# A decoder trunk's weight streams: which gate pairs take seven products, where the single weight block lies, and the order of a product's last pair

## The chip, the cores and the metric

The kernel runs on one core of one Trainium2 chip. The metric is the device time of one execution in microseconds (us), lower is better. A matrix product here is done by TensorE (PE), the weights are prepared by ScalarE (ACT) and VectorE (DVE), GpSimd (POOL) does a few element-wise steps, and SyncE (SP) issues the transfers.

## The reference

One layer of a decoder, 256 tokens, width D = 2048, all in float32. In short:

```python
h = rms_norm(x, mix_norm)
proj = h @ w_in                      # q, k, v of two attentions, LRU, SSM, and 4 * 2048 gate columns
branches = [dilated(proj), lru(proj), sliding(proj), ssm(proj)]      # four mixers, 768 wide each
merged = sum(sigmoid(gate_b) * (branch_b @ w_branch[b]) for b in range(4))
x2 = x + merged @ w_out
u = rms_norm(x2, ffn_norm)
out = x2 + (silu(u @ w_gate) * (u @ w_up)) @ w_ffn_out               # hidden width 5632
```

## The kernel before, in words

The 256 tokens are two blocks t = 0, 1 of 128. Weights come once from HBM, 1 MB at a time. The activations stand in SBUF transposed, each split into a high and a low part; every weight block is split likewise: ACT writes the high part `wh` (L209) and DVE the rest `wl` (L214). One product of a weight block with an activation block is three matmuls of 128x128 by 128x512 (L202 high by high, L203 high by low weight, L204 low by high weight).

`stream_pairs` multiplies by two column blocks n = 0, 1 of 512, so a product has four results (n, t), each one bank of PSUM. A pair p is one 1 MB transfer: two row blocks k = 0, 1 of the two column blocks. `plan` is the order of the pairs. An ordinary pair makes two weight blocks a (k = 0) and b (k = 1) of 128x1024 and does eight products, `for k, n, t`. A pair in `seven` does seven products in their place, in the manner of Strassen and Winograd: from the raw weights DVE makes a sum t13 (L227, `ws`) and two more sums (L233, L234), and the weight blocks are a (one block, 128x512), b, c (of t13) and d (of the last two sums), each 128x1024 but a. The seven products go to three of the four result banks and to four shared banks m1, m5, m7, m6, which are added in at the end of the pairs of that kind (`shared_products`). The operands on the activation side (`hs_hi`, `hs_lo` for the gates, from `input_sums`; `xs` and `sx` for the FFN) are formed once.

Raw weights have 3 buffers, `whi` and `wlo` 4 each, whatever the block's size. A slot comes free when the last product with its block is done.

The last pair of every product is done bank by bank, so that bank (0,0) is finished first, then (0,1), (1,0), (1,1):

```python
                order = [(k, n, t) for k in range(2) for n in range(2) for t in range(T)]
                if i == len(plan) - 1:
                    order = [(k, n, t) for n in range(2) for t in range(T) for k in range(2)]
```

PSUM has eight banks: `psm` holds two tiles of two banks, `psx` four single banks (tag `mps`). A product in `psm` takes both of the two tiles, one for each n, so the next one in `psm` needs the same four banks again. A dependence goes by the tile: a read of one bank of a tile waits for both, and the next product's first matmul in a tile waits for the reads of both.

The stages in the order of time: start, SSM, LRU and attention projections up to 587 us; eight gates (c = 0, 1, four mixers each), each followed by its branch product of three pairs (in `psx` banks), to 1062.9; `w_out` (`stream`) to 1154.7; eleven products of the first FFN matrix (`w_ffn_in`, j = 0 to 10, 43.2 us each); two products of the second one (`w_ffn_out`, c = 0 from 1630.1, c = 1 from 1750.1). The gate product is read by DVE at L973, the branch at L983, the FFN-in product at L1078 (n = 0) and L1082 (n = 1), the second matrix's at L1145. Eight pairs a gate; eight pairs, two of them with seven products, in an FFN-in product; 22 pairs, eight with seven products, in one of the second matrix.

The gates use `PLAN_GATE`: gate (0, 0) has no pair of seven, (0, 1) and (1, 0) have a plan of their own, the five others take the pairs in order 0 to 7; seven gates have pairs 1, 3, 5 with seven products.

The order on each engine is set by Tile's scheduler, ahead of the run. The weights' loads, splits and sums stand in `tc.high_priority(offset=4000)`, the reads of the banks don't. Between pairs `pump()` advances side work (transposes, sums, loads of operands) held in two queues, near and far, as generators.

Two small tables are loaded among the constants at the start: `tri`, a mask of the SSM, and `onehot`, the distance table from which `bias_vector` makes the attention bias with one matmul.

Of the kernel before, what the change touches and what calls it, by code (L numbers as in the profile page):

```python
# [10 lines left out]
F32 = mybir.dt.float32  # L11
F32R = mybir.dt.float32r
AF = mybir.ActivationFunctionType
ALU = mybir.AluOpType
# [4 lines left out]
P = 128  # L19
D = 2048  # L20
S = 256
T = S // P
# [4 lines left out]
KG = 2  # L27
# [10 lines left out]
UNITS = [("c", 0), ("c", 1)] + [("a", h) for h in range(6)]  # L38
LINE = 512
SB_LOW, SB_TOP = 16512, 212960  # L40
CONST = 4640
SEVEN_GATE = (1, 3, 5)
PLAN_GATE = {(0, 0): (range(8), ()), (0, 1): ((0, 2, 1, 4, 3, 6, 5, 7), SEVEN_GATE), (1, 0): ((0, 2, 1, 4, 3, 6, 5, 7), SEVEN_GATE)}
SEVEN_IN = (3, 5)
SEVEN_OUT = list(range(1, 16, 2))
PLAN_OUT = ([0, 2, 4, 6, 1, 8, 3, 10, 5, 12, 7, 14, 9, 16, 11, 17, 13, 18, 15, 19, 20, 21], list(range(22)))
# [36 lines left out]
def hybrid(ctx, tc, a):  # L83
    nc = tc.nc
    V, A, G, PE = nc.vector, nc.scalar, nc.gpsimd, nc.tensor
# [8 lines left out]
    wp = ctx.enter_context(tc.tile_pool(name="wp", bufs=4))  # L94
    actp = ctx.enter_context(tc.tile_pool(name="actp", bufs=1))
    const = ctx.enter_context(tc.tile_pool(name="const", bufs=1))
    pad("pad_c", -CONST % LINE)
    psm = ctx.enter_context(tc.tile_pool(name="psm", bufs=2, space=PSUM))
# [3 lines left out]
    def ctile(shape, name, src=None, dt=F32):  # L102
        t = const.tile(shape, dt, name=name, tag=name)
        if src is not None:
            nc.sync.dma_start(t, src)
        return t

    def mps(name):
        return psx.tile([P, 512], F32, name=name, tag="mps")
# [16 lines left out]
    def pump():  # L126
        for queue in side.values():
            advance(queue)
# [45 lines left out]
    def stream_pairs(src, offset, plan, hi, lo, seven, name, mid=None, pool="psm"):  # L174

        if pool == "psm":  # L180
            two = [psm.tile([P, T, 512], F32, name=f"ps_{name}_{n}", tag="psmain") for n in range(2)]
            c = [[two[n][:, t] for t in range(T)] for n in range(2)]
        else:
            c = [[mps(f"ps_{name}_{n}{t}") for t in range(T)] for n in range(2)]
        m = {}
        left, begun = {}, set()

        def banks(p):
            if p in seven:
                return ["m1", (0, 0), (1, 0), "m5", "m7", "m6", (0, 1)]  # L190
            return [(n, t) for _ in range(2) for n in range(2) for t in range(T)]

        for p in plan:
            for b in banks(p):
                left[b] = left.get(b, 0) + 1

        def product(b, x, w, z):
            xh, xl = x
            wh, wl = w
            out = m[b] if b in m else c[b[0]][b[1]]  # L200
            left[b] -= 1
            PE.matmul(out, xh, wh[:, z], start=b not in begun, stop=False)  # L202
            PE.matmul(out, xh, wl[:, z], start=False, stop=False)  # L203
            PE.matmul(out, xl, wh[:, z], start=False, stop=left[b] == 0)  # L204
            begun.add(b)

        def high(x, z0, z1, nm):
            wh = wp.tile([P, KG, 512], F32R, name=f"wh_{nm}", tag="whi")
            A.activation(wh[:, z0:z1], x, AF.Copy)  # L209
            return x, z0, z1, wh, nm  # L210

        def low(x, z0, z1, wh, nm):
            wl = wp.tile([P, KG, 512], F32R, name=f"wl_{nm}", tag="wlo")
            V.tensor_tensor(wl[:, z0:z1], x, wh[:, z0:z1].bitcast(F32), op=ALU.subtract)  # L214
            return wh, wl

        sevens = [i for i, p in enumerate(plan) if p in seven]
        for i, p in enumerate(plan):
            with tc.high_priority(offset=4000):
                raw = wp.tile([P, 4, 512], F32, name=f"wr_{name}_{p}", tag="wraw", bufs=RAW)  # L220
                o = offset + p * P * 4 * 512
                nc.sync.dma_start(
                    raw, bass.AP(tensor=src.tensor, offset=src.offset + o, ap=[[4 * 512, P], [512, 4], [1, 512]])
                )
                if p in seven:
                    t13 = pools["sum"].tile([P, 2, 512], F32, name=f"ws_{name}_{p}", tag="wsum")
                    V.tensor_tensor(t13, raw[:, 1:3], raw[:, 0:1].to_broadcast([P, 2, 512]), op=ALU.add)  # L227
                    h11 = high(raw[:, 1:2], 1, 2, f"{name}_{p}a")
                    h2 = high(raw[:, 2:4], 0, 2, f"{name}_{p}b")
                    h13 = high(t13, 0, 2, f"{name}_{p}c")  # L230
                    w11 = low(*h11)
                    w2 = low(*h2)
                    V.tensor_tensor(raw[:, 0], t13[:, 1], raw[:, 1], op=ALU.add)  # L233
                    V.tensor_tensor(raw[:, 1], raw[:, 3], raw[:, 0], op=ALU.add)  # L234
                    h24 = high(raw[:, 0:2], 0, 2, f"{name}_{p}d")
                    w13 = low(*h13)
                    w24 = low(*h24)
                else:
                    w1 = low(*high(raw[:, 0:2], 0, 2, f"{name}_{p}a"))
                    w2 = low(*high(raw[:, 2:4], 0, 2, f"{name}_{p}b"))  # L240

            def x(k, t):
                return hi[:, 2 * p + k, t * P : (t + 1) * P], lo[:, 2 * p + k, t * P : (t + 1) * P]

            if p in seven:
                if not m:
                    m = {b: mps(f"{b}_{name}") for b in ("m1", "m5", "m7", "m6")}
                s = [(h[0][:, h[2], j], h[1][:, h[2], j]) for h in (seven[p],) for j in range(3)]
                product("m1", x(0, 0), w11, 1)
                product((0, 0), x(1, 0), w2, 1)  # L250
                product((1, 0), x(0, 1), w2, 0)
                product("m5", s[0], w13, 0)
                product("m7", s[2], w13, 1)
                product("m6", s[1], w24, 0)
                product((0, 1), x(1, 1), w24, 1)
                if i == sevens[-1]:
                    mid(m)
            else:
                order = [(k, n, t) for k in range(2) for n in range(2) for t in range(T)]
                if i == len(plan) - 1:  # L260
                    order = [(k, n, t) for n in range(2) for t in range(T) for k in range(2)]
                for z, (k, n, t) in enumerate(order):
                    product((n, t), x(k, t), (w1, w2)[k], 1 - n)
                    if z == 3 and pool == "psm" and not (sevens and sevens[0] < i < sevens[-1]):
                        pump()
            if i < len(plan) - 1 and pool == "psm" and not (sevens and sevens[0] <= i < sevens[-1]):
                pump()
        return c
# [79 lines left out]
    for kind, j, sl in chunk_plan():  # L348
        n = sum(w for _, w in sl)
# [12 lines left out]


    ident = ctile([P, P], "ident", a["ident"])
    tri = ctile([P, P], "tri", a["tri"])
    ones = ctile([P, P], "ones")
    V.memset(ones, 1.0)
    scw = ctile([P, 10, 5], "scw", a["conv_ssm"])
# [24 lines left out]
    tabx = ctile([36, 24], "tabx")  # L393
    nc.sync.dma_start(tabx[0:32, :], a["rel_bias_table"])
    nc.sync.dma_start(tabx[32:36, :], a["group_neg"])
    onehot = ctile([36, 384], "onehot", a["onehot"])
    bvec = dram.tile([24, 384], F32, name="bvec", tag="bvec")

    def bias_vector():
        bps = mps("bias_ps")  # L400
        PE.matmul(bps[:24, :384], tabx, onehot, start=True, stop=True)
        bsb = aq.tile([P, 512], F32, name="bsb", tag="tok", bufs=3)
        V.tensor_copy(bsb[:24, :384], bps[:24, :384])
        nc.sync.dma_start(bvec, bsb[:24, :384])
        yield
# [42 lines left out]
    aq = att1.enter_context(tc.tile_pool(name="aq", bufs=1, side="right"))  # L448
# [3 lines left out]
    sp_ = ssd.enter_context(tc.tile_pool(name="sp_", bufs=1, side="right"))  # L452
# [24 lines left out]

    zz = sp_.tile([P, T, BW], F32, name="zz", tag="zz")
    dtx = sp_.tile([P, T, 12], F32, name="dtx", tag="dtx")
    xbcT = sp_.tile([P, 10, S + 3], F32, name="xbcT", tag="xbcT")  # L480
    V.memset(xbcT[:, :, 0:3], 0.0)
    cv = sp_.tile([P, 10, S], F32, name="cv", tag="cv")
# [267 lines left out]
    pools = {}  # L750
# [168 lines left out]
    order = (1, 3, 2, 0)  # L919
# [25 lines left out]
    def input_sums():  # L945
        for i, p in enumerate(SEVEN_GATE):
            s3 = slice(2 * p, 2 * p + 2)
# [7 lines left out]
    for c in range(2):  # L955
        mg = gmp.tile([P, 2, T, 512], F32, name=f"mg{c}", tag="mg")
        for ib, b in enumerate(order):
            g4 = gmp.tile([P, 2, T, 512], F32, name=f"gt{c}{b}", tag="gt")
            gt = [[g4[:, n, t] for t in range(T)] for n in range(2)]
            if (c, ib) == (0, 1):  # L960
                mtp_stack, mT_hi, mT_lo = close_attention()
                hp = pools["sum"] = hsum.enter_context(tc.tile_pool(name="hp", bufs=1, side="right"))
                hs_hi, hs_lo = (hp.tile([P, len(SEVEN_GATE), 3, P], F32R, name=f"hs_{x}", tag=f"hs_{x}") for x in ("hi", "lo"))
                later(input_sums(), "far")
            plan, sv = PLAN_GATE.get((c, ib), (range(8), SEVEN_GATE))
            sv = {p: (hs_hi, hs_lo, SEVEN_GATE.index(p)) for p in sv}
            gps = stream_pairs(
                win, gate_off + (c * 4 + ib) * D * 1024, plan, actA_hi, actA_lo, sv, f"g{c}{b}", lambda m, gt=gt: shared_products(m, gt)
# [117 lines left out]
    n = len(SEVEN_OUT)  # L1086
# [159 lines left out]
```

## Time and profile before

| | |
|---|---|
| time, median of 3 runs | 1870.43 us (1869.89 to 1871.45) |
| time of the profiled execution | 1871.93 us |
| span of the profiled execution | 1870.2 us |
| mean granted TensorE clock | 0.999 |
| TensorE matmuls busy | 1854.8 us |
| VectorE busy | 1429.9 us |
| ScalarE busy | 970.6 us |
| HBM traffic | 195 GB/s over the span |

The span is the stretch from the first to the last instruction that the profiler recorded; the execution's own time is a little longer. A row of busy time counts how long instructions of an engine were open. Matmuls overlap one another, so the sum over matmuls is longer than what each adds to the end; the starts of one after another tell that.

### The profile page before, as it was taken

The numbers are of one execution on the slowest core, as the hardware profiler recorded it, in microseconds if no ns is written. First come the engines' busy times: TensorE is split into PE (matmuls) and PEld (weight loads), VectorE is DVE, ScalarE is ACT, GpSimd is POOL, SyncE is SP. The second block draws the span as 40 slices with busy tenths as digits, with TensorE's granted clock in tenths as the row PEclk, the third lists the DMA queues.
The fourth block names the chain that finished last, engine by engine and source line by source line (L and its number), as shares of the span: only waits on it lengthen the run. The fifth ranks groups of instructions, "written<-read, shape, count | busy, mean of one in ns | idle before, by whom it ended". The sixth has DMA issues, their size and how long they took to land.

```text
span 1870.2 us, 22270 instructions
## 1 busy us (share of the span) xinstructions
PE 1854.8 (99%) x8537; PEld 1543.9 (83%) x8537; DVE 1429.9 (76%) x1766; ACT 970.6 (52%) x1220; POOL 175.1 (9%) x152
## 2 busy tenths in 40 slices
PE   8999999999999999999999999999999999999998
PEld 8988888888888888888888888888888888878887
DVE  6867876565555788888888766888888888888885
ACT  6645655444444455555555554555555555455553
POOL 0032422222122001110011100000000000000000
PEclk9999999999999999999999999999999999999999
DMA  8644454455444455455556656445555555555653
GB/s 297 208 158 154 179 198 174 166 180 187 168 178 169 173 196 199 187 190 216 196 197 226 222 180 225 185 185 209 204 188 213 213 196 198 195 207 217 247 196 142
DMA packets 64392, 365.47 MB, mean 195 GB/s; under 512 B 7904, under 2 KB 19484, under 8 KB 23196
## 3 DMA queue, kind: packets, MB, share of 16 engines
q1 hardware_dynamic: 64284, 364.04, 53.1%
q8 instruction: 67, 1.10, 0.2%
q14 instruction: 41, 0.34, 0.1%
HBM read 358.21 MB, written 5.80 MB: 195 GB/s over the span
## 4 chain that ended last, share of the span: by engine, by line
PE 93%; DVE 3%; issue 2%; DMA 2%; ACT 0%; POOL 0%; DVEq 0%; POOLq 0%; ACTq 0%
PE ps_fi L202 7%; PE ps_fi L204 7%; PE ps_fi L203 7%; PE ps_att L169 6%; PE ps_att L167 6%; PE ps_att L168 6%; PE ps_g L202 5%; PE ps_g L204 5%; PE ps_g L203 5%; PE ps_fo L202 3%; PE ps_fo L203 3%; PE ps_fo L204 3%; PE ps_b L204 2%; PE ps_b L202 2%; PE ps_b L203 2%
## 5 line engine op out<-in xcount | busy, mean ns | idle before, releaser
L161 DVE TENSOR_TENSOR wl_att<-wr_att,wh_att 128x1024 fp32r<-128x1024 f32 x128 | 159.6, 1250 | 92.5 <-ACT wh_att L159 92.3
L159 ACT ACTIVATE wh_att<-wr_att 128x1024 fp32r<-128x1024 f32 x128 | 135.4, 1059 | 163.9 <-PE ps_att L169 145.3
L167 PE MATMUL ps_att<-wh_att,hT_hi 128*128 128x512 f32 x512 | 206.3, 403 | 0.0
L169 PE MATMUL ps_att<-wh_att,hT_lo 128*128 128x512 f32 x512 | 200.0, 391 | 0.0
L168 PE MATMUL ps_att<-wl_att,hT_hi 128*128 128x512 f32 x512 | 199.5, 390 | 0.0
L169 PEld LDWEIGHTS ps_att<-wh_att,hT_lo 128*128 128x128 f32 x512 | 96.1, 188 | 20.7
L168 PEld LDWEIGHTS ps_att<-wl_att,hT_hi 128*128 128x128 f32 x512 | 96.4, 188 | 19.0
L167 PEld LDWEIGHTS ps_att<-wh_att,hT_hi 128*128 128x128 f32 x512 | 96.3, 188 | 18.8
L985 POOL TENSOR_TENSOR mg<-mg,gt 128x512 f32<-128x512 f32 x24 | 38.7, 1642 | 434.3 <-DVE gt L983 434.3
L167 PE MATMUL ps_ssm<-wh_ssm,hT_hi 128*128 128x384 f32 (+2 forms) x160 | 57.2, 358 | 7.0 <-ACT hT_hi L312 7.0
L161 DVE TENSOR_TENSOR wl_o<-wr_o,wh_o 128x1024 fp32r<-128x1024 f32 x32 | 40.8, 1281 | 24.8 <-ACT wh_o L159 24.7
L159 ACT ACTIVATE wh_o<-wr_o 128x1024 fp32r<-128x1024 f32 x32 | 33.8, 1061 | 47.0 <-PE ps_o L169 38.6
L790 POOL TENSOR_TENSOR sq_t<-tk_t 128x512 f32<-128x512 f32 (+3 forms) x32 | 32.5, 1025 | 272.2 <-ACT tk_t L785 271.9
L168 PE MATMUL ps_ssm<-wl_ssm,hT_hi 128*128 128x384 f32 (+2 forms) x160 | 56.7, 355 | 0.6 <-DVE wl_ssm L161 0.6
L169 PE MATMUL ps_ssm<-wh_ssm,hT_lo 128*128 128x384 f32 (+2 forms) x160 | 56.5, 353 | 0.0
L167 PE MATMUL ps_o<-wh_o,mT_hi 128*128 128x512 f32 x128 | 50.8, 397 | 0.0
L169 PE MATMUL ps_o<-wh_o,mT_lo 128*128 128x512 f32 x128 | 50.0, 390 | 0.0
L168 PE MATMUL ps_o<-wl_o,mT_hi 128*128 128x512 f32 x128 | 49.8, 389 | 0.0
L159 ACT ACTIVATE wh_ssm<-wr_ssm 128x768 fp32r<-128x768 f32 (+2 forms) x40 | 35.2, 889 | 26.9 <-PE ps_ssm L169 16.9
L161 DVE TENSOR_TENSOR wl_ssm<-wr_ssm,wh_ssm 128x768 fp32r<-128x768 f32 (+2 forms) x40 | 40.2, 1012 | 9.9 <-ACT wh_ssm L159 9.7
L159 ACT ACTIVATE wh_lru<-wr_lru 128x1024 fp32r<-128x1024 f32 x24 | 25.4, 1059 | 29.2 <-PE ps_lru L169 21.0
L167 PE MATMUL ps_lru<-wh_lru,hT_hi 128*128 128x512 f32 x96 | 39.3, 409 | 0.0
(1235 smaller groups left out, 5622.0 us busy)
## 6 DMA issues: line engine op xcount, KB each, us to landing
wr_fi<-in_w_ffn_in SPq DMA_DIRECT2D x88, 1024.0 KB, 4.8
wr_att<-in_w_in SPq DMA_DIRECT2D x64, 1024.0 KB, 4.7
wr_g<-in_w_in SPq DMA_DIRECT2D x64, 1024.0 KB, 4.8
wr_fo<-in_w_ffn_out SPq DMA_DIRECT2D x44, 1024.0 KB, 4.9
wr_b<-in_w_branch SPq DMA_DIRECT2D x24, 1024.0 KB, 4.8
wr_o<-in_w_out SPq DMA_DIRECT2D x16, 1024.0 KB, 4.8
wr_lru<-in_w_in SPq DMA_DIRECT2D x12, 1024.0 KB, 4.8
wr_ssm<-in_w_in SPq DMA_DIRECT2D x8, 768.0 KB, 6.5
```

Source lines behind the costliest of these rows:

```text
L159: A.activation(wh, rk, AF.Copy)
L161: V.tensor_tensor(wl, rk, wh.bitcast(F32), op=ALU.subtract)
L167: PE.matmul(o_ps, xh, wh[:, kk], start=(k == 0), stop=False)
L168: PE.matmul(o_ps, xh, wl[:, kk], start=False, stop=False)
L169: PE.matmul(o_ps, xl, wh[:, kk], start=False, stop=(k == kc - 1))
L202: PE.matmul(out, xh, wh[:, z], start=b not in begun, stop=False)
L203: PE.matmul(out, xh, wl[:, z], start=False, stop=False)
L204: PE.matmul(out, xl, wh[:, z], start=False, stop=left[b] == 0)
L790: G.tensor_tensor(sq[:, :m], tok[:, :m], tok[:, :m], op=ALU.mult)
L985: G.tensor_tensor(mg[:, n, t], mg[:, n, t], gt[n][t], op=ALU.add)
```

## The change

Five edits.

1. Pair 7 joins pairs 1, 3 and 5: four of eight pairs have seven products in the seven gates that have such pairs. `input_sums` forms a fourth set of operands.
2. The plans change: (0, 1) and (1, 0) go 0, 2, 1, 3, 4, 5, 7, 6; the five other gates go 1, 0, 3, 2, 5, 4, 7, 6. Each of these ends in an ordinary pair.
3. The single weight block (a of a pair of seven) gets one buffer of its own for its high part and one for its low part (`wh1`, `wl1`), in the gates and in both FFN matrices, instead of a slot of `whi` and `wlo`.
4. The last pair's own order goes: it is done like the others, weight block by weight block, in every product of `stream_pairs`.
5. `tri` and `onehot` leave the constants and are loaded later, into pools of the SSM and the attention; the constants shrink from 4640 to 2592 bytes.

```diff
-CONST = 4640
-SEVEN_GATE = (1, 3, 5)
-PLAN_GATE = {(0, 0): (range(8), ()), (0, 1): ((0, 2, 1, 4, 3, 6, 5, 7), SEVEN_GATE), (1, 0): ((0, 2, 1, 4, 3, 6, 5, 7), SEVEN_GATE)}
+CONST = 2592
+SEVEN_GATE = (1, 3, 5, 7)
+PLAN_GATE = {
+    (0, 0): (range(8), ()),
+    (0, 1): ((0, 2, 1, 3, 4, 5, 7, 6), SEVEN_GATE),
+    (1, 0): ((0, 2, 1, 3, 4, 5, 7, 6), SEVEN_GATE),
+}
...
-        def high(x, z0, z1, nm):
-            wh = wp.tile([P, KG, 512], F32R, name=f"wh_{nm}", tag="whi")
-            A.activation(wh[:, z0:z1], x, AF.Copy)
-            return x, z0, z1, wh, nm
+        def high(x, nm):
+            if x.shape[1] == 1:
+                wh = pools["sum"].tile([P, 1, 512], F32R, name=f"wh_{nm}", tag="wh1")
+            else:
+                wh = wp.tile([P, KG, 512], F32R, name=f"wh_{nm}", tag="whi")
+            A.activation(wh, x, AF.Copy)
+            return x, wh, nm
...
+        def low(x, wh, nm):
+            if x.shape[1] == 1:
+                wl = pools["sum"].tile([P, 1, 512], F32R, name=f"wl_{nm}", tag="wl1")
+            else:
+                wl = wp.tile([P, KG, 512], F32R, name=f"wl_{nm}", tag="wlo")
+            V.tensor_tensor(wl, x, wh.bitcast(F32), op=ALU.subtract)
             return wh, wl
...
-                product("m1", x(0, 0), w11, 1)
+                product("m1", x(0, 0), w11, 0)
...
                 order = [(k, n, t) for k in range(2) for n in range(2) for t in range(T)]
-                if i == len(plan) - 1:
-                    order = [(k, n, t) for n in range(2) for t in range(T) for k in range(2)]
...
-    tri = ctile([P, P], "tri", a["tri"])
...
-    onehot = ctile([36, 384], "onehot", a["onehot"])
...
     def bias_vector():
+        onehot = aq.tile([P, 512], F32, name="onehot", tag="tok", bufs=3)[:36, :384]
+        nc.sync.dma_start(onehot, a["onehot"])
+        yield
         bps = mps("bias_ps")
...
+    tri = sp_.tile([P, P], F32, name="tri", tag="tri")
+    nc.sync.dma_start(tri, a["tri"])
...
-            plan, sv = PLAN_GATE.get((c, ib), (range(8), SEVEN_GATE))
+            plan, sv = PLAN_GATE.get((c, ib), ((1, 0, 3, 2, 5, 4, 7, 6), SEVEN_GATE))
```

## Rows read from the trace of the kernel before

**Rows 1.** The page's busy times, share of the span, instructions.

```profile
PE 1854.8 (99%) x8537; PEld 1543.9 (83%) x8537; DVE 1429.9 (76%) x1766; ACT 970.6 (52%) x1220; POOL 175.1 (9%) x152
```

**Rows 2.** The waits of TensorE: us in total, times, longest.

```profile
PE ps_ssm L167 <- ACT hT_hi L312: 7.0, 1, 7.0
PE m_fo L203 <- DVE wl_fo_1d L214: 1.3, 1, 1.3
PE m_fo L202 <- ACT wh_fo_1d L209: 0.8, 1, 0.8
```

**Rows 3.** Windows: length, busy time of PE, PEld, DVE, ACT, POOL, granted clock, DMA share, GB/s.

```profile
946.00:1004.00 58.00, 57.72 (x255) 47.50 (x254) 48.09 (x49) 30.46 (x34) 6.39 (x5) 1.00 0.53 198
...
1154.00:1630.00 476.00, 476.00 (x2138) 392.39 (x2138) 405.61 (x484) 254.51 (x295) 1.08 (x1) 1.00 0.54 203
...
1660.40:1664.00 3.60, 3.60 (x11) 2.81 (x10) 3.60 (x5) 1.79 (x2) 0.00 (x0) 0.53 0.90 344
...
1811.00:1815.00 4.00, 4.00 (x19) 3.26 (x19) 4.00 (x5) 1.11 (x2) 0.00 (x0) 1.00 0.80 287
```

**Rows 4.** The timeline of TensorE: start, length, instruction; one product.

```profile
893.63 0.39 PE L202 MATMUL m_g<-wh_g_1a,hT_hi 128*128 128x512 f32 x1
...
894.31 0.39 PE L202 MATMUL ps_g<-wh_g_1b,hT_hi 128*128 128x512 f32 x1
```

**Rows 5.** The timeline of TensorE: block d of pairs of seven in the gates.

```profile
720.83 0.39 PE L202 MATMUL m_g<-wh_g_1d,hs_hi 128*128 128x512 f32 x1
...
721.50 0.40 PE L204 MATMUL m_g<-wh_g_1d,hs_lo 128*128 128x512 f32 x1
...
954.83 0.39 PE L202 MATMUL m_g<-wh_g_1d,hs_hi 128*128 128x512 f32 x1
...
955.83 0.39 PE L204 MATMUL m_g<-wh_g_1d,hs_lo 128*128 128x512 f32 x1
...
1023.70 0.39 PE L202 MATMUL m_g<-wh_g_3d,hs_hi 128*128 128x512 f32 x1
...
1024.57 0.39 PE L204 MATMUL m_g<-wh_g_3d,hs_lo 128*128 128x512 f32 x1
```

**Rows 6.** The timeline of TensorE: from one FFN-in product to the next.

```profile
1281.61 0.39 PE L202 MATMUL ps_fi<-wh_fi_7a,x2T_hi 128*128 128x512 f32 x1
...
1284.33 0.39 PE L202 MATMUL ps_fi<-wh_fi_0a,x2T_hi 128*128 128x512 f32 x1
...
1289.32 0.47 PE L202 MATMUL ps_fi<-wh_fi_0a,x2T_hi 128*128 128x512 f32 x1
```

**Rows 7.** The timeline of VectorE there.

```profile
1281.81 1.29 DVE L1078 TENSOR_TENSOR sa<-ps_fi,sa 128x512 f32<-128x512 f32 x2 [0.40 <-PE ps_fi L204]
...
1285.14 1.22 DVE L214 TENSOR_TENSOR wl_fi_1a<-wr_fi,wh_fi_1a 128x1024 fp32r<-128x1024 f32 x1
```

**Rows 8.** The timeline of ScalarE, there and at the opening of ffn_out.

```profile
1283.90 1.06 ACT L209 ACTIVATE wh_fi_1a<-wr_fi 128x1024 fp32r<-128x1024 f32 x1
...
1655.44 0.85 ACT L285 ACTIVATE sx_hi<-sr 128x768 fp32r<-128x768 f32 x1 [3.97 <-DMA sr<-sums]
```

**Rows 9.** The timeline of VectorE from a gate to its branch.

```profile
753.94 0.69 DVE L973 TENSOR_TENSOR gt<-ps_g,gt 128x512 f32<-128x512 f32 x1 [1.43 <-PE ps_g L204]
754.55 1.22 DVE L214 TENSOR_TENSOR wl_b_1a<-wr_b,wh_b_1a 128x1024 fp32r<-128x1024 f32 x1
...
756.82 0.68 DVE L973 TENSOR_TENSOR gt<-ps_g,gt 128x512 f32<-128x512 f32 x1
```

**Rows 10.** The timeline of TensorE in ffn_out: block d of two pairs of seven.

```profile
1656.10 0.39 PE L204 MATMUL m_fo<-wh_fo_1c,sx_lo 128*128 128x512 f32 x1
...
1659.07 0.50 PE L203 MATMUL m_fo<-wl_fo_1d,sx_hi 128*128 128x512 f32 x1 [1.29 <-DVE wl_fo_1d L214]
...
1810.06 0.39 PE L202 MATMUL m_fo<-wh_fo_11d,sx_hi 128*128 128x512 f32 x1
1810.76 0.50 PE L203 MATMUL m_fo<-wl_fo_11d,sx_hi 128*128 128x512 f32 x1 [0.31 <-DVE wl_fo_11d L214]
```

More of the change, by code (lines that the diff above doesn't have):

```diff
@@ L205, in product @@
             begun.add(b)
-        def high(x, z0, z1, nm):
-            wh = wp.tile([P, KG, 512], F32R, name=f"wh_{nm}", tag="whi")
-            A.activation(wh[:, z0:z1], x, AF.Copy)
-            return x, z0, z1, wh, nm
-        def low(x, z0, z1, wh, nm):
-            wl = wp.tile([P, KG, 512], F32R, name=f"wl_{nm}", tag="wlo")
-            V.tensor_tensor(wl[:, z0:z1], x, wh[:, z0:z1].bitcast(F32), op=ALU.subtract)
+        def high(x, nm):
[11 more added lines that the diff above has]
+            V.tensor_tensor(wl, x, wh.bitcast(F32), op=ALU.subtract)
             return wh, wl
@@ L227, in stream_pairs @@
                     V.tensor_tensor(t13, raw[:, 1:3], raw[:, 0:1].to_broadcast([P, 2, 512]), op=ALU.add)
-                    h11 = high(raw[:, 1:2], 1, 2, f"{name}_{p}a")
-                    h2 = high(raw[:, 2:4], 0, 2, f"{name}_{p}b")
-                    h13 = high(t13, 0, 2, f"{name}_{p}c")
+                    h11 = high(raw[:, 1:2], f"{name}_{p}a")
+                    h2 = high(raw[:, 2:4], f"{name}_{p}b")
+                    h13 = high(t13, f"{name}_{p}c")
                     w11 = low(*h11)
@@ L234, in stream_pairs @@
                     V.tensor_tensor(raw[:, 1], raw[:, 3], raw[:, 0], op=ALU.add)
-                    h24 = high(raw[:, 0:2], 0, 2, f"{name}_{p}d")
+                    h24 = high(raw[:, 0:2], f"{name}_{p}d")
                     w13 = low(*h13)
@@ L238, in stream_pairs @@
                 else:
-                    w1 = low(*high(raw[:, 0:2], 0, 2, f"{name}_{p}a"))
-                    w2 = low(*high(raw[:, 2:4], 0, 2, f"{name}_{p}b"))
+                    w1 = low(*high(raw[:, 0:2], f"{name}_{p}a"))
+                    w2 = low(*high(raw[:, 2:4], f"{name}_{p}b"))
             def x(k, t):
```

## The prediction

> **What bounds the kernel now.** I read the page's busy times first, then what TensorE waits for, then stretches of the span, and at last single instructions around the edit. TensorE is busy 1854.8 of 1870.2 us [rows 1], and of its waits 7.0 us are the start; the next are 1.3 and 0.8 us, both for one weight block [rows 2]. The reader is to see that nothing is left to gain but matmuls taken out and a few short stalls, and that any new stall on TensorE goes straight to the end. VectorE comes next: 48.09 of 58 us in a gate with its branch, 405.61 of 476 in the first FFN matrix [rows 3]. The clock is granted in full in both stretches.
>
> Busy time is no price for a matmul: three of them stand as one product in the rows, each 0.39 us long, but the next product starts 0.68 us after [rows 4]. So the pitch is 0.227 us a matmul, 0.68 a product. A stall below is what a gap between starts has over 0.227.
>
> **1. The fourth pair of seven products.** Seven gates each lose one product of eight in one pair: 7 × 0.68 = 4.76 us less. What the pair adds runs on other engines: VectorE works on four double blocks and three single ones instead of two double blocks, 4 × 1.22 [rows 7] + 3 × 0.69 [rows 9] = 6.95 against 2.44, 4.5 us more: 52.6 of 57 us in a gate, up from 48.09 of 58 [rows 3]. That cover is thin, and in (0,1) and (1,0), where two pairs of seven now follow each other, I allow 0 to 2 us. The fourth operand sum (seven short vector instructions, at most 7 × 0.69 = 4.8 us, once) runs beside the first gates' products. If the cover were gone, the 4.5 us would come onto TensorE in each gate, 7 × 4.5 = 31 us; the rows leave 4.4 us to spare, so I take 0.
>
> **2. Late blocks in the gates that run pairs 0 to 7 in order.** There the last weight block (d) of a pair of seven, mostly the first one, comes late: from its first to its third matmul 0.67, 1.00 and 0.87 us pass where two pitches are 0.45 [rows 5]. Five such places in four gates (three shown, the two between of 0.27 us each) make 0.22 + 0.55 + 0.42 + 0.54 = 1.7 us. After, the single block (a) has buffers of its own, so one slot of the four is saved before d, and the pair comes first in the plan, behind a branch that leaves VectorE and ScalarE time. I take −1.7; the bounds are 0 (it is late as now) and −1.7.
>
> **3. The order of the last pair.** This is the term that decides. Where one product follows another directly in the same four banks (ten times from one FFN-in product to the next, once into ffn_out, once between its two halves: 12 places), the next product's n=0 tile is the buffer of the last one's n=0 tile, and its first matmul waits until both banks of it are read out. Before, the bank-by-bank order ends tile 0 at 1281.61, four products ahead of the boundary at 1284.33 [rows 6]. VectorE reads it from 1281.81 to 1283.10 [rows 7], and TensorE goes on without a gap: 4.99 us from 1284.33 to 1289.32 are 22 pitches.
> After, the second weight block's four products come last, and of these the first two fill tile 0. It is complete 2 × 0.68 = 1.36 us ahead of the boundary E instead of 2.72, so at E − 1.16 it can be read (0.20 after the next product's start, as at 1281.81). Two reads take 1.29 us together. If VectorE were free, they would end at E + 0.13, and with 0.1 us to the matmul the stall is 0.23 us.
> But it isn't free. The first weight block's slot, held until E − 0.68 now (its ACT split starts at 1283.90, 0.25 later [rows 8]), is free at E − 2.72. So the split for the next pair's block starts at E − 2.5, ends at E − 1.46, and VectorE's half (1.22 us at 1285.14 [rows 7]) is ready at E − 1.43, 0.27 us before the read. Weights go first where both wait: at the end of a gate one bank of a tile is read at 753.94 and its other bank, ready as early, at 756.82, after two weight blocks [rows 9]. Then wl runs −1.43 to −0.30, the reads to +1.00, TensorE starts at E + 1.09. Before there is no gap but 0.08 us at the n=1 tile, whose matmul at 1289.32 is 0.47 long instead of 0.39 [rows 6], and that goes: 12 × 1.01 = +12.1 us. The bounds are the two orders: 12 × 0.15 = 1.9 and, if the split starts a little later or something short comes between the reads, 12 × 1.2 = 14.4. I take 12.1, because the row of 756.82 is nearest to it and because the weights are ready first.
> Tile 1 is complete at E, as now, and is read by E + 4.67 where 5.44 us of n=0 work stand ahead of it: no stall there. Eight gates and eight branches change order too, but a gate's banks are not asked for again until its branch has passed, and a branch's are four others.
> The Trainium skill (Perfetto Trace Analysis, Matmuls) asks that groups of matmuls rotate through banks so that one group's evacuation overlaps the next one's matmuls. The trace agrees: that is what the bank-by-bank order gives at 1281.81. By the rule the new order costs something at each of the 12 places; it names no size.
>
> **4. The opening of ffn_out.** From 1656.10 to 1659.07 two pitches take 2.97 us [rows 10]: 2.5 us of stall on block d of pair 1. Its ACT split stands behind an operand split that waited 3.97 us for a DMA until 1655.44 [rows 8]. Right after, the clock is granted at 0.53 for 3.60 us [rows 3], which loses 3.60 × 0.47 = 1.7 us; 4.2 in all. The slot for d comes free about 2.7 us earlier after, but the DMA that stands ahead on ScalarE is not touched. Bounds 0 and −4.2; I take −1.5, nearer to none, as the DMA ends last.
>
> **5. Other d blocks.** At 1810.06 to 1810.76 the gap is 0.47 us over a pitch [rows 10]; the own buffer should give it back: −0.5 (0 to −0.8 with its smaller like in the first half).
>
> **6. Moved loads.** The mask and the one-hot table are loaded later into other pools, one more yield before the bias matmul. SP's queue gets both out of the constants' row; a late one-hot would hold one small matmul and what stands behind it on TensorE. By the nearest row, a wait of 3.97 us for a DMA [rows 8], the bounds are 0 and +4; a gain at the start is excluded, since its wait [rows 2] is for the input, whose loads are issued ahead of the constants. I take +0.2: the load has a yield's time, about a pair of products, to land, and one pump more costs little.
>
> **Sum:** −4.76 − 1.7 + 12.1 − 1.5 − 0.5 + 0.2 = +3.8 us. The profiled execution took 1871.93 (span 1870.2 and 1.73 around it), the median is 1870.43, 1.5 lower; on that median the sum gives 1874.3.
>
> **The rivals.**
> A, the forecast: weights first at the 12 places. Its own range comes from terms 1, 3, 4 and 6: full relief at ffn_out gives 1871.6, none with sevens late by 2 us 1878. Chance 0.68.
> B, the other side: VectorE takes the two bank reads before the weight block. For it: reads at 1281.81 go at once, and the two are only 0.27 us apart, so a slightly slower split turns it. Against it: [rows 9]. It decides from the point where the read is ready before the split, and gives 12 × 0.15 = 1.9 in place of 12.1: −4.76 − 1.7 + 1.9 − 1.5 − 0.5 + 0.2 = −6.4, so 1864.1, and 1861.4 with the full 4.2 at ffn_out. Chance 0.24.
> C, VectorE becomes the bound in the gates: 48.09 of 58 us and 4.4 more leave 5, but in bursts; 1 us at each of seven gates gives 1874.3 + 7 = 1881. Chance 0.05.
> D, the clock: stalls of 1.09 us in every FFN-in product might halve it as at 1660.40, at 1.7 us each: 12 × 1.7 = 20 more, 1895. Against it: after the gap at 1810.06 the clock stays at full [rows 3], and the drop came after stalls of 2.5 us. Chance 0.03. The Trainium skill (TensorE: Matmul & The Clock Gate, A second HAM failure mode) tells of a kernel whose engine idled briefly between groups and swung between half and full clock; by that D would hold, and no row here shows a swing after a gap of 1 us.
> That the change does nothing (the products leave and the time stays) has no place to hide 4.76 us at 99% busy.
>
> **How the numbers follow.** A change within 0.2% (3.7 us, about what a measurement here can tell) reaches to 1874.2, right at A's value: half of A, 0.33, counts as the same and as much as slower, which with C and D makes 0.41. B is faster, with 0.02 of A for less stall and full relief together: 0.26. The range runs from 1863 (B at its likeliest, with part of the relief) to 1878.5 (A at its worst, and a little), leaving out C, D and B's far end. A's own range is 1871.6 to 1878.
>
> **What would show it.** Right: gaps of about 1.1 us on TensorE at every boundary of two FFN-in products, released by the reads of bank tile 0, with wl_fi_1a just ahead of them on VectorE; 0.68 us less in each of seven gates; no gap at d in a gate's pairs of seven. Wrong: the reads stand ahead of wl_fi_1a and the gap is 0.2 us (then B), a clock under 1.0 between 1154 and 1630 (D), or gates of 58 us with TensorE waiting for wl (C).

## The result, and the profile after

The changed kernel takes 1892.36 us (median of 4 runs, 1890.83 to 1892.53) against 1870.43: a ratio of 1.0118, 95% interval 1.0106 to 1.0130. It is 22 us slower; 1874.3 was forecast, in a range up to 1878.5. The profiled execution took 1892.53, its span is 1890.8.

The page's busy times of the changed kernel answer to [rows 1]:

```profile
PE 1856.2 (98%) x8516; PEld 1541.0 (82%) x8516; DVE 1458.5 (77%) x1808; ACT 985.5 (52%) x1236; POOL 183.1 (10%) x152
```

The engines are hardly busier, the span is 20.6 us longer. So nearly all of the time went into waits, and a little into half clock (below). These are TensorE's waits, in us, times and the longest one, to be held against [rows 2]:

```profile
PE ps_fi L206 <- DVE sa L1089: 9.8, 10, 1.0
PE m_g L206 <- DVE gt L994: 8.7, 8, 1.8
PE ps_ssm L171 <- ACT hT_hi L320: 7.1, 1, 7.1
```

Ten waits of 1.0 us at the FFN-in boundaries are new, and eight in the gates, of which the longest is 1.8. The two at ffn_out in [rows 2] are gone. Where the time lies in the span is told by the first matmul of each stage; the stages' lengths in us, worked out from those starts:

| from one stage's first matmul to the next's | before | after | difference |
|---|---|---|---|
| start to the first gate | 587.45 | 587.37 | −0.1 |
| eight gates and branches | 475.45 | 487.17 | +11.7 |
| w_out | 91.84 | 91.84 | 0 |
| FFN-in | 475.36 | 487.82 | +12.5 |
| ffn_out, to the start of the last matmul | 234.75 | 230.65 | −4.1 |
| from there to the end of the span | 5.3 | 5.9 | +0.6 |

Of ffn_out's 234.75 us before, 1.7 are the half clock at 1660.40 [rows 3], which most executions of that kernel don't hold: it lowers the mean granted clock by 0.0009, and nine of the 15 that stand beside experiments 5 to 8 show a mean of 1.000. Without it the −4.1 in the table is −2.4.

**FFN-in.** TensorE's timeline at a boundary, to be held against [rows 6], then VectorE's there, against [rows 7]:

```profile
1298.02 0.39 PE L208 MATMUL ps_fi<-wh_fi_7b,x2T_lo 128*128 128x512 f32 x1
1299.39 0.47 PE L206 MATMUL ps_fi<-wh_fi_0a,x2T_hi 128*128 128x512 f32 x1 [0.98 <-DVE sa L1089]
```

```profile
1296.82 1.23 DVE L224 TENSOR_TENSOR wl_fi_1a<-wr_fi,wh_fi_1a 128x1024 fp32r<-128x1024 f32 x1 [1.50 <-ACT wh_fi_1a L216]
1297.97 1.28 DVE L1089 TENSOR_TENSOR sa<-ps_fi,sa 128x512 f32<-128x512 f32 x2
```

The start-to-start gap is 1.37 us, 1.14 over a pitch, and the same ten times. Block 1a's low part runs first, then the two reads, whose end releases TensorE. This is case A of the prediction, which gave 1.09.

**The gates.** TensorE in gate (0, 2): the first matmul of block d of the first pair in the plan, into a shared bank, waits for VectorE's L994.

```profile
720.04 0.49 PE L207 MATMUL ps_g<-wl_g_0b,hT_hi 128*128 128x512 f32 x1
722.36 0.50 PE L206 MATMUL m_g<-wh_g_1d,hs_hi 128*128 128x512 f32 x1 [1.84 <-DVE gt L994]
```

VectorE's timeline from the end of the branch (712.24 is the gate's first matmul):

```profile
712.28 1.79 DVE L243 TENSOR_TENSOR wr_g<-ws_g,wr_g 128x512 f32<-128x512 f32 x1
713.99 1.27 DVE L994 SCALAR_TENSOR_TENSOR gt<-gt,ps_b 128x512 f32<-128x512 f32 x2
715.19 1.94 DVE L224 TENSOR_TENSOR wl_g_0a<-wr_g,wh_g_0a 128x1024 fp32r<-128x1024 f32 x1
717.05 1.78 DVE L224 TENSOR_TENSOR wl_g_3a<-wr_g,wh_g_3a 128x512 fp32r<-128x512 f32 x1
718.76 1.21 DVE L224 TENSOR_TENSOR wl_g_0b<-wr_g,wh_g_0b 128x1024 fp32r<-128x1024 f32 x1
719.89 1.21 DVE L224 TENSOR_TENSOR wl_g_3b<-wr_g,wh_g_3b 128x1024 fp32r<-128x1024 f32 x1
721.03 0.68 DVE L244 TENSOR_TENSOR wr_g<-wr_g 128x512 f32<-128x512 f32 x1
721.63 0.68 DVE L994 SCALAR_TENSOR_TENSOR gt<-gt,ps_b 128x512 f32<-128x512 f32 x1
```

L994 is the read of a branch's bank (L983 before the change). Three of the four are done by 715.3, and the fourth, whose bank's last matmul begins at 712.01, comes at 721.63, after four weight blocks and a sum. TensorE takes up d at 722.36. The reader should also see the durations: 1.79, 1.94 and 1.78 us for instructions that take 0.69, 1.22 and 0.69 elsewhere, until 718.8; from there on they are as usual. GpSimd's timeline shows what ran beside them:

```profile
711.30 2.21 POOL L996 TENSOR_TENSOR mg<-mg,gt 128x512 f32<-128x512 f32 x1 [117.57 <-DVE gt L994]
714.75 3.53 POOL L996 TENSOR_TENSOR mg<-mg,gt 128x512 f32<-128x512 f32 x2 [1.23 <-DVE gt L994]
```

It ends these three additions at 718.3. VectorE's instructions follow one another without a pause: it doesn't stand idle for GpSimd, its instructions themselves take longer beside it. The same gap, 2.05 to 2.10 us over a pitch, stands in four gates: (0, 2), (0, 3), (1, 2) and (1, 3). Behind two of them, in these windows (columns as in [rows 3]), the clock was at half for part of the stretch, behind the other two it was not:

```profile
722.40:726.00 3.60, 3.60 (x11) 2.86 (x12) 2.59 (x3) 1.06 (x1) 2.18 (x1) 0.64 0.42 175
784.16:788.00 3.84, 3.84 (x10) 2.98 (x11) 2.73 (x3) 1.06 (x1) 2.13 (x1) 0.59 0.41 171
963.04:967.00 3.96, 3.96 (x17) 3.27 (x18) 2.93 (x3) 1.65 (x2) 2.21 (x1) 1.00 0.43 180
1024.50:1028.50 4.00, 3.95 (x17) 3.30 (x18) 2.36 (x2) 1.69 (x2) 2.15 (x1) 1.00 0.47 193
```

Gate (1, 1) has the same plan and no such gap. It follows the first branch of its half, whose result goes to `mg` without an addition on GpSimd. There VectorE has the same order and full speed:

```profile
895.80 0.68 DVE L243 TENSOR_TENSOR wr_g<-ws_g,wr_g 128x512 f32<-128x512 f32 x1
896.40 1.28 DVE L994 SCALAR_TENSOR_TENSOR mg<-gt,ps_b 128x512 f32<-128x512 f32 x2
897.60 1.22 DVE L224 TENSOR_TENSOR wl_g_0a<-wr_g,wh_g_0a 128x1024 fp32r<-128x1024 f32 x1
898.73 0.69 DVE L224 TENSOR_TENSOR wl_g_3a<-wr_g,wh_g_3a 128x512 fp32r<-128x512 f32 x1
...
902.21 0.68 DVE L994 SCALAR_TENSOR_TENSOR mg<-gt,ps_b 128x512 f32<-128x512 f32 x1
```

The fourth read starts 6.46 us after the gate's first matmul (895.75) there, 9.39 after it in (0, 2). Of the 2.93 us between, the three slowed instructions make 1.10 + 0.72 + 1.09 = 2.91.

### The profile page after: what moved, and what is told of

It is laid out like the page before. It is cut to its first block, busy times and chain, and to the rows that moved or that the text cites. A ratio compares the mean times of both kernels' runs of the same rounds, so it can differ in the third digit from the quotient of the medians.

```text
span 1890.8 us, 22282 instructions
## 1 busy us (share of the span) xinstructions
PE 1856.2 (98%) x8516; PEld 1541.0 (82%) x8516; DVE 1458.5 (77%) x1808; ACT 985.5 (52%) x1236; POOL 183.1 (10%) x152
## 4 chain that ended last, share of the span: by engine, by line
PE 89%; DVE 7%; DMA 2%; ACT 1%; issue 1%; SPq 0%; POOL 0%; DVEq 0%; ACTq 0%; POOLq 0%
PE ps_fi L206 7%; PE ps_fi L208 7%; PE ps_fi L207 7%; PE ps_att L173 6%; PE ps_att L171 6%; PE ps_att L172 6%; PE ps_g L208 4%; PE ps_g L207 4%; PE ps_g L206 4%; PE ps_fo L206 3%; PE ps_fo L207 3%; PE ps_fo L208 3%; PE ps_o L171 2%; PE ps_o L173 2%; PE ps_o L172 2%; PE ps_ssm L171 1%
## 5 line engine op out<-in xcount | busy, mean ns | idle before, releaser
L996 POOL TENSOR_TENSOR mg<-mg,gt 128x512 f32<-128x512 f32 x24 | 46.7, 1959 | 441.0 <-DVE gt L994 441.0
```

What stands on the lines that cost most here:

```text
L996: G.tensor_tensor(mg[:, n, t], mg[:, n, t], gt[n][t], op=ALU.add)
```

## The experiments

All comparisons are with runs of the kernel before on the same chip. The stretches named are the stages of the table above.

**1. GpSimd's additions left out.** The edit removes, of the changed kernel,

```diff
-                    if ib:
-                        G.tensor_tensor(mg[:, n, t], mg[:, n, t], gt[n][t], op=ALU.add)
```

> Left out: GpSimd's sums of the four branches (24 instructions), so the merged activations are those of one branch. VectorE's order of instructions stays the same. Theory T (block d waits for a branch bank whose last read stands behind five weight instructions on VectorE, and these are slowed while GpSimd runs): the weight instructions fall from 1.8 and 1.9 us back to 0.7 and 1.2, the four gaps of about 2.1 us at d and the half clock behind them go, 11 to 14 us less, about 1879 to 1881; the ten FFN gaps of 1.14 stay. Rival O (the order on VectorE alone): the gaps shrink by under half, 1887 or more. Rival V (VectorE has too much to do with four pairs of seven): they stay, 1890 or more.

Measured: 1875.97 us against 1869.57, ratio 1.0034 (1.0021 to 1.0048); the gates take 471.67 us, 15.5 less than in the changed kernel, FFN-in 488.08. VectorE in gate (0, 2), in the same order of instructions (here the gate begins 0.8 us earlier, at 711.43):

```profile
711.83 0.68 DVE L243 TENSOR_TENSOR wr_g<-ws_g,wr_g 128x512 f32<-128x512 f32 x1
712.43 1.27 DVE L994 SCALAR_TENSOR_TENSOR gt<-gt,ps_b 128x512 f32<-128x512 f32 x2
713.63 1.22 DVE L224 TENSOR_TENSOR wl_g_0a<-wr_g,wh_g_0a 128x1024 fp32r<-128x1024 f32 x1
714.76 0.68 DVE L224 TENSOR_TENSOR wl_g_3a<-wr_g,wh_g_3a 128x512 fp32r<-128x512 f32 x1
...
718.24 0.68 DVE L994 SCALAR_TENSOR_TENSOR gt<-gt,ps_b 128x512 f32<-128x512 f32 x1
```

The long durations are gone, the fourth read starts 6.81 us after the gate's first matmul instead of 9.39, and the gap at d shrinks from 2.10 to 0.29 us. Theory T holds; the relief is a little larger than it said, since the smaller gaps at block c (0.54 in three gates, 1.35 in one) went too, but for 0.22. V and O fall. What is shown is that these 24 instructions slow VectorE and that without the slowing the gaps all but go. It is not the only condition: in experiments 3 and 4 GpSimd still adds, and the gaps at d go as well when the read starts earlier.

The Trainium skill (GPSIMD Engine Reference, Specifications) says that GpSimd shares VectorE's way to SBUF and that this is felt by VectorE's instructions with two inputs from SBUF. The trace agrees: L243 and L224, with two such inputs, take 1.78 us beside GpSimd instead of 0.69, while L994, one of whose inputs is a PSUM bank, takes 0.68 in either case.

**2. The old order of the last pair.** In the changed kernel,

```diff
                 order = [(k, n, t) for k in range(2) for n in range(2) for t in range(T)]
+                if i == len(plan) - 1:
+                    order = [(k, n, t) for n in range(2) for t in range(T) for k in range(2)]
```

> The changed kernel with the last pair bank by bank again, everywhere. T: the ten gaps of 1.14 us between FFN-in products and the one into ffn_out go, 12.5 us less, about 1880; the four gaps at d stay near 2 us, since the branch's last bank is finished at the same moment. Rival L (the new order makes the branch's banks late, and so the gate gaps): these go as well, 12.5 + 14, about 1866.

Measured: 1876.47 against 1869.57, ratio 1.0039 (1.0024 to 1.0054). FFN-in takes 482.69, the gates 477.57. Both expectations for FFN-in were too low: the gaps of 1.14 at the boundary are gone, but a gap of 0.71 at the n = 1 tile has come in their place, ten times:

```profile
1204.71 0.39 PE L208 MATMUL ps_fi<-wh_fi_1b,x2T_lo 128*128 128x512 f32 x1
1205.65 0.50 PE L206 MATMUL ps_fi<-wh_fi_0a,x2T_hi 128*128 128x512 f32 x1 [0.55 <-DVE ua L1095]
```

It waits for L1095, the second read of `ua`. In the gates four gates keep two gaps each, of 0.80 us for a weight block that GpSimd slows (2.31 us for 1.22) and of 0.97 at d; these gates take 42.88 us, where 60 products without a gap take 40.80. Against the 469.17 of experiment 7 the gates lose 8.4 us here and 18.0 in the changed kernel: about half is left, and neither T (all stays) nor L (all goes) had the size.

**3. An ordinary pair first in five gates.**

```diff
-            plan, sv = PLAN_GATE.get((c, ib), ((1, 0, 3, 2, 5, 4, 7, 6), SEVEN_GATE))
+            plan, sv = PLAN_GATE.get((c, ib), ((0, 1, 2, 3, 4, 5, 7, 6), SEVEN_GATE))
```

> The changed kernel with an ordinary pair first in the five gates (0, 1, 2, 3, 4, 5, 7, 6), four pairs of seven kept. T: the gates no longer ask for a branch's banks in their first 5 us; gaps at d go, the stretch of gates falls from 487 to about 469 to 472 us, about 1874 to 1878; FFN gaps stay at 1.14. Rival V (too much for VectorE with four pairs of seven): gaps stay somewhere in the gates, 1885 or more.

Measured: 1876.70 against 1869.57, ratio 1.0041 (1.0026 to 1.0056). The gates take 471.18, 16.0 less than in the changed kernel, and five gates are 40.80 us, which is 60 products of 0.68 without a gap. FFN-in keeps its 488.10. T's time holds, and V falls once more: four pairs of seven fit. But the plan acts in another way than T says. VectorE and TensorE in gate (0, 2), whose first matmul is at 711.25:

```profile
714.65 0.68 DVE L994 SCALAR_TENSOR_TENSOR gt<-gt,ps_b 128x512 f32<-128x512 f32 x1
720.09 0.39 PE L206 MATMUL m_g<-wh_g_1d,hs_hi 128*128 128x512 f32 x1
```

Block d asks for the fourth bank 8.84 us into the gate. In the changed kernel its turn on TensorE came at 8.03 (720.04 and a pitch, from 712.24), so the need has moved by 0.8 us only. The fourth read has moved by 6: it starts 3.40 us into the gate instead of 9.39, with one weight block between it and the third read instead of four and a sum. Why VectorE has fewer blocks ahead of it there was not tested.

**4. The branch's reads ahead of the weights.**

```diff
-                    V.scalar_tensor_tensor(dst, gt[n][t], 1.0, bps[n][t], op0=ALU.add, op1=ALU.mult)
+                    with tc.high_priority(offset=8000):
+                        V.scalar_tensor_tensor(dst, gt[n][t], 1.0, bps[n][t], op0=ALU.add, op1=ALU.mult)
```

> The changed kernel with the reads of the branch's banks put ahead of the weight instructions on VectorE (a higher priority for these 32 instructions). T: the banks are free in time, the gaps at d go, a weight block may come up to 0.7 us late in their place: 10 to 14 us less, about 1879 to 1883. Rival V: 1888 or more, as the weight blocks are late instead.

Measured: 1880.57 against 1869.57, ratio 1.0059 (1.0042 to 1.0075). The gates take 477.13, 10 less. The gaps at d are gone in the four gates; a weight block comes 0.5 to 0.6 us late in three, and gate (1, 0) takes 46.95 instead of 43.67, as its shared banks now wait for the transposes' reads (L949) for 0.8 and 1.6 us, behind which the clock is at half from 847.6 to 851.0. T's time, with part of the gain given back at a place that neither theory named.

**5. The own buffer alone, on the kernel before.**

```diff
+            if z0:
+                z0, z1 = 0, 1
+                wh = pools["sum"].tile([P, 1, 512], F32R, name=f"wh_{nm}", tag="wh1")
...
+            if z1 == 1:
+                wl = pools["sum"].tile([P, 1, 512], F32R, name=f"wl_{nm}", tag="wl1")
...
-                product("m1", x(0, 0), w11, 1)
+                product("m1", x(0, 0), w11, 0)
```

> The kernel before with the single weight block in buffers of its own, nothing else. Theory W (the own buffer lets VectorE take block a of the next pair and its sums ahead of the second read of ua, as in the run with the old order): a gap of about 0.7 us at each of ten FFN-in boundaries, FFN-in 482.7 instead of 475.4; the second matrix 229 to 230 instead of 234.7, gates about 1 less: 1 us more in all, about 1871. Rival F (a buffer more costs nothing): FFN-in stays at 475.4, about 1864.

Measured: 1872.93 against 1869.43, ratio 1.0017 (1.0008 to 1.0026). FFN-in takes 482.56, ffn_out 229.77, the gates 474.35. VectorE behind a boundary:

```profile
1283.90 0.69 DVE L1089 TENSOR_TENSOR ua<-ps_fi,ua 128x512 f32<-128x512 f32 x1
1284.51 1.22 DVE L221 TENSOR_TENSOR wl_fi_1a<-wr_fi,wh_fi_1a 128x1024 fp32r<-128x1024 f32 x1
1285.64 1.22 DVE L221 TENSOR_TENSOR wl_fi_1b<-wr_fi,wh_fi_1b 128x1024 fp32r<-128x1024 f32 x1
1286.78 1.22 DVE L234 TENSOR_TENSOR ws_fi<-wr_fi 128x1024 f32<-128x1024 f32 x1
1287.91 0.69 DVE L221 TENSOR_TENSOR wl_fi_3a<-wr_fi,wh_fi_3a 128x512 fp32r<-128x512 f32 x1
1288.52 0.68 DVE L240 TENSOR_TENSOR wr_fi<-ws_fi,wr_fi 128x512 f32<-128x512 f32 x1
1289.12 0.68 DVE L1089 TENSOR_TENSOR ua<-ps_fi,ua 128x512 f32<-128x512 f32 x1
```

Between the two reads of `ua` stand five instructions, where the kernel before has three (from 1285.14 in [rows 7], the second read at 1288.54): block 3a and a sum (L240) come ahead as well, since 3a no longer waits for a slot. W holds, F falls: a buffer more lets work go ahead that TensorE doesn't need yet, and the read that it does need is late by 0.71 us. The three stages sum to 1.1 us more than in the profile before, whose ffn_out holds the 1.7 us of half clock; the medians differ by 3.5.

**6. The new order alone, on the kernel before.** The two lines of the last pair's order are removed, nothing else.

> The kernel before with the last pair weight block by weight block, nothing else. The theory of the prediction (case A): wl_fi_1a ahead of the two reads on VectorE, gaps of about 1.1 us at ten FFN-in boundaries and the one into ffn_out, 12 to 13 us more, about 1883; gates as before, with at most small gaps. Rival F2: the gaps need the own buffer as well, and it stays at 1870 to 1873.

Measured: 1883.43 against 1869.43, ratio 1.0071 (1.0057 to 1.0085). FFN-in takes 487.75, and VectorE shows case A without the own buffer:

```profile
1287.41 1.23 DVE L214 TENSOR_TENSOR wl_fi_1a<-wr_fi,wh_fi_1a 128x1024 fp32r<-128x1024 f32 x1 [1.49 <-ACT wh_fi_1a L209]
1288.55 1.28 DVE L1076 TENSOR_TENSOR sa<-ps_fi,sa 128x512 f32<-128x512 f32 x2
```

Rival F2 falls. The gates take 478.23, 2.8 more than before, with gaps of 0.85 at d in four gates, which this expectation had as small. They are not those of the changed kernel: TensorE waits for a weight block there and not for a bank, whose fourth read starts 3.45 us into the gate.

```profile
721.36 0.50 PE L203 MATMUL m_g<-wl_g_1d,hs_hi 128*128 128x512 f32 x1 [0.69 <-DVE wl_g_1d L214]
```

ffn_out takes 229.74 here too, without the own buffer.

**7. What remains when the losses are taken out.** The own buffer stays in the gates and in ffn_out alone (`if x.shape[1] == 1 and name[:2] != "fi":`), with the old order of the last pair and the plan of experiment 3.

> The changed kernel with the last pair bank by bank, an ordinary pair first in five gates, and the own buffer in the gates and the second matrix alone. T and W together: gates about 470 to 471 (before 475.4), FFN-in 475.4 as before, the second matrix 229.4 (before 234.7): 9 to 10 us less than before, 1860 to 1862. If the gain of the gates or of the second matrix needs the order or FFN-in's buffers: 1866 or more.

Measured: 1861.23 against 1869.43, ratio 0.9954 (0.9940 to 0.9967). The windows of FFN-in and ffn_out show TensorE without a gap:

```profile
1149.10:1624.50 475.40, 475.40 (x2135) 391.75 (x2134) 405.26 (x483) 254.59 (x295) 1.08 (x1) 1.00 0.55 203
1624.50:1854.00 229.50, 229.50 (x1017) 189.63 (x1015) 188.38 (x199) 120.72 (x126) 0.00 (x0) 1.00 0.59 207
```

Gates 469.17, FFN-in 475.40, ffn_out 229.42: as expected, the gates a little better.

**8. The own buffer everywhere, FFN-in's reads first.** As the last, but the four reads of an FFN-in product (of `sa` and `ua`) stand in `tc.high_priority(offset=8000)`, and the own buffer stays.

> As the last, but the own buffer stays everywhere, and FFN-in's reads of its banks get a higher priority than the weights (44 instructions). W: the ten gaps of 0.7 go, since the second read of ua no longer stands behind five instructions: 1860 to 1862. Rival V2 (VectorE can't do both in time, a weight block is late in place of the read): FFN-in 479 or more, 1864 or more.

Measured: 1861.12 against 1869.43, ratio 0.9953 (0.9940 to 0.9965); FFN-in 475.31, with no gap at its boundaries, and ffn_out 230.67, with one of 0.84 us for a weight block. W holds: it is the place of the read on VectorE that made experiment 2's and 5's gaps.

**9. Half a block ahead of the reads.** The plan of experiment 3, the new order kept, the reads with a higher priority, and in FFN-in

```diff
+                    if name[:2] == "fi" and i == 1:
...
+                        for z in range(2):
+                            V.tensor_tensor(wl[:, z], raw[:, z], wh[:, z].bitcast(F32), op=ALU.subtract)
```

> The changed kernel (its new order of the last pair kept) with an ordinary pair first in five gates, and in FFN-in VectorE's part of block 1a in two halves of about 0.6 us and the reads of the banks with a higher priority: half a block stands ahead of the reads instead of a whole one. The theory of the prediction (the gap is what VectorE has ahead of two reads that can start at E - 1.16): the gaps fall from 1.14 to about 0.55 us, FFN-in from 488.1 to about 482, 6 less than the run with an ordinary pair first, about 1870. Rival K (the gap is a fixed cost of finishing and reading a tile so late): 1.14 stays, about 1876.

Measured: 1871.74 against 1868.73, ratio 1.0016 (1.0006 to 1.0025); FFN-in 482.88. VectorE and TensorE at a boundary:

```profile
1280.94 0.69 DVE L253 TENSOR_TENSOR wl_fi_1a<-wr_fi,wh_fi_1a 128x512 fp32r<-128x512 f32 x1 [1.49 <-ACT wh_fi_1a L216]
1281.55 1.28 DVE L1097 TENSOR_TENSOR sa<-ps_fi,sa 128x512 f32<-128x512 f32 x2
...
1283.94 0.68 DVE L253 TENSOR_TENSOR wl_fi_1a<-wr_fi,wh_fi_1a 128x512 fp32r<-128x512 f32 x1
```

```profile
1282.14 0.39 PE L208 MATMUL ps_fi<-wh_fi_7b,x2T_lo 128*128 128x512 f32 x1
1282.97 0.47 PE L206 MATMUL ps_fi<-wh_fi_0a,x2T_hi 128*128 128x512 f32 x1 [0.45 <-DVE sa L1097]
```

The gap is 0.61 us over a pitch, where the prediction's reckoning, carried over in the expectation, gives 0.55. K falls: the gap goes with the length of what stands ahead of the reads.

**10. Three pairs of seven in the best version.** `SEVEN_GATE = (1, 3, 5)` and the old plans of (0, 1) and (1, 0) in the kernel of experiment 7.

> The best version so far (own buffer not in FFN-in, old order of the last pair, an ordinary pair first) with pairs 1, 3, 5 alone in seven products. Term 1 of the prediction: seven products more, 7 x 0.68 = 4.76 us, about 1866, gates of 41.48 instead of 40.80. Rival N (the fourth pair's work on VectorE eats its gain): within 1.5 of 1861.

Measured: 1865.68 against 1868.73, ratio 0.9985 (0.9976 to 0.9995). Gates of 41.48 us stand against 40.80, and the stretch of gates takes 474.46 against 469.17, 5.3 us for the 4.76 of term 1. N falls.

## Why the prediction was wrong

Of the 18.1 us between the forecast and the result, the gates make 18.2 (−6.5 forecast, +11.7 measured); the other terms nearly cancel.

**Term 3, the boundaries, was right in mechanism and nearly in size.** Forecast were 12 gaps of 1.09 us with block 1a ahead of the reads; ten of 1.14, one of 1.10 into ffn_out and one of 0.46 between its halves came, and rival B (the reads first) did not. The reckoning from [rows 7 to 9] carried over to half a block in experiment 9. Two slips in it change nothing: 12 × 0.15 is 1.8 and not 1.9, and the n = 0 work ahead of tile 1 is 4.99 us in [rows 6] and 4.40 in the changed kernel, not 5.44.

**The step that failed is the sentence behind it:** "a gate's banks are not asked for again until its branch has passed, and a branch's are four others". A branch's four banks are those that the next gate's shared results m1, m5, m7 and m6 take. In a plan that begins with pair 0, the gate needs the first of them only after eight products, 5.4 us; with a pair of seven first it needs one at once and, as TensorE's order stands, the fourth 8.0 us in. The fourth branch read, meanwhile, stands behind weight blocks and starts 9.39 us in, where it starts 3.40 us in with an ordinary pair first (experiment 3). So the plan brings the need a little forward and makes the read come far later. I weighed that rule, weights ahead of reads, for the FFN's banks and not for these. Term 2 went wrong with it: "the pair comes first in the plan, behind a branch that leaves VectorE and ScalarE time" took the place for a gain of 1.7 us. The other half of term 2, the own buffer, was right: alone (experiment 5) it takes 1.6 us off those four gates. Terms 1 and 2 together were to save 6.5 us in the gates; 11.7 were lost. Without the plan the gates take 471.18 (experiment 3), without the new order 477.57 (experiment 2), without both 469.17 (experiment 7): the plan costs 8.4 us by itself, the new order 2.0 (1.0 each in (0, 1) and (1, 0), none in the other five), and together they cost 18.0. With both, the fourth read starts 9.39 us into a gate instead of 8.46 with the plan alone, the second at 1.75 us instead of 1.21 before its first matmul, so that block c waits too, and the clock falls behind two of the gaps; how the 7.6 us more divide among these was not taken apart.

**A second thing was missing from the sum:** that VectorE's instructions take 0.7 to 1.1 us longer while GpSimd adds. The profile before had it nowhere in the rows that I chose. But its trace shows it in gate (0, 2), beside GpSimd's additions from 709.81 to 716.30:

```profile
715.06 1.79 DVE L234 TENSOR_TENSOR wr_g<-wr_g 128x512 f32<-128x512 f32 x1
```

It is what turns a read that is late but in time (6.46 us behind, in gate (1, 1)) into one that stalls TensorE. Experiment 1 takes it away and the gates fall to 471.67.

**Rival C** had the right place (the gates, with TensorE waiting for VectorE) and a time of 1881, but the wrong mechanism: VectorE has room for four pairs of seven, as gates of exactly 40.80 us show. It was priced by VectorE's total and not by what a certain read stands behind.

**Rival D**, the clock, didn't hold at the FFN's gaps of 1.14 us: from 1166 to 1652 the granted clock is 1.00. It showed at gaps of 2.1 us, behind two of four, (0, 2) and (0, 3) at 45.43 and 45.46 us against (1, 2) at 43.83 without it: 1.6 us each, near the 1.7 of the row at 1660.40.

**Term 1** was right: gates of 40.80 us in experiments 3 and 7 stand against 41.48 in experiments 5 and 10.

**Terms 4 and 5** were mis-sized: −2.0 forecast, −4.1 measured, and about −5 in experiments 5 and 7, 1.7 of each being the half clock at 1660.40; the stalls' part is 2.4 and 3.3. The step that failed is "the DMA that stands ahead on ScalarE is not touched". The DMA isn't, but the order on ScalarE is. Block d's split now comes ahead of the operand split, to be held against [rows 8]:

```profile
1674.57 1.07 ACT L216 ACTIVATE wh_fo_1d<-wr_fo 128x1024 fp32r<-128x1024 f32 x1 [1.71 <-PE ps_fo L208]
...
1679.42 0.85 ACT L293 ACTIVATE sx_hi<-sr 128x768 fp32r<-128x768 f32 x1 [0.55 <-DMA sr<-sums]
```

The same came about with the own buffer alone (experiment 5) and with the new order alone (experiment 6), so either of them is enough; why the scheduler puts it so stays open.

**Term 6** was right within what can be told: the start is 0.1 us shorter, the end 0.6 longer.

The gap of about 0.6 us at block d in gate (1, 0), which waits for a read of the transposes and is in the best version too, was not pursued.

## What to carry to other kernels

When work is moved to the front of a stage, list every bank and buffer that it asks for, and for each one who holds it, and behind what its last read stands on its engine; a priority for weights means that such a read comes after every weight that is ready. An extra buffer is not free in an ordered queue: it lets later work pass in front of a read that another engine is waiting for (7.2 us in FFN-in), so give it only where a wait for the slot shows, or raise the read's priority with it. When a plan is changed, see where it moves a read and not only where it moves the need: here the read moved by 6 us and the need by 0.8. Test the parts of a change on their own: of this one, the fourth pair of seven gains some 5 us and the own buffer some 3 in ffn_out, while the order of the last pair alone loses 14 in all.

## What the runs showed of the hardware that was not expected

- VectorE instructions with two SBUF inputs took up to 1.79 us instead of 0.69 (128x512) and up to 2.35 instead of 1.22 (128x1024) while GpSimd added in SBUF; those that read a PSUM bank kept their 0.68 (16 of them lie wholly beside GpSimd's additions in experiment 3). GpSimd's additions took longer as well: 1.96 us on average against 1.64 before.
- After gaps of 2.05 to 2.10 us the granted clock fell to half behind two of four, and stayed full behind ten of 1.14 us. In experiment 4 it fell behind gaps of 0.77 and 1.63 us that lay 2.4 us apart; in experiment 9 it stayed full behind one of 1.63 in ffn_out, at 1781.43.
